# A hybrid decoder layer on one core: the gates of a block regrouped, small PE work queued behind the products before it

## The chip, the cores and the metric

One core of a Trainium2 chip runs the whole program. The metric is the device time of one execution in microseconds (us). Engines are named as in the profile: PE is TensorE (matrix products), DVE is VectorE, ACT is ScalarE, POOL is GpSimd, SP is SyncE, which only issues DMAs here.

## The reference

One layer of a decoder trunk on 1024 prompt tokens and 32 sample tokens, 1056 columns T in all. Two token mixers (latent attention and a state-space layer) run first; then comes the part in question, a gated FFN with a width-3 convolution and a per-layer embedding:

```python
x = x + mixed @ w_out
up = rmsnorm(x, g_ffn) @ w_up                     # 1024 -> 2 x 2816, then a causal conv of width 3
a, v = split(conv(up), 2)
x = x + (gelu(a) * v) @ w_down                    # 2816 -> 1024
x = x + sigmoid(rmsnorm(x, g_ple) @ w_ple_gate) * (p @ w_ple_proj)
```

The last two rows of `up` per sequence are an output of their own (`conv_prompt`, `conv_sample`).

## The kernel before, in words

Everything is kept transposed: 128 channels on the partitions, tokens along the free dimension. Products are made in fp32r, with each operand split into a high and a low part; `mm3` (lines 85 to 88) does three matmuls for one product (high x high, high x low, low x high).

The up projection runs over 22 pairs of row blocks in `up_pair`. Each pair's gelu(a) * v is written to memory (`dhid`, line 2069) and read back later. The last stage is `block(b)` for three blocks of 352 tokens. Each block has a down stage and a gate stage:

- down: 8 outputs `o`, each the sum over 22 hidden row blocks, into a PSUM tile `pd`; `down_out` (lines 2156 to 2167) adds it to the residual `xb`, makes the scaled high and low parts `gg` for the gates, and adds the squares into `sqb`;
- gate: 8 outputs, each 8 row blocks of `gg` times w_ple_gate, 24 matmuls into a PSUM tile `pu`. After gate 0, `sums` (line 2196) adds `sqb` over the partitions with six small matmuls and takes a reciprocal square root; after gate 1, `rows` (line 2208) spreads it along the partitions with three transposes, into `rb`. `rest(o)` (lines 2222 to 2225) multiplies the gate by `rb`, applies the sigmoid, multiplies by `pe` and adds `xb`. `out_turn(o)` (lines 2232 to 2240) transposes the result y with three PE transposes, copies it on ACT and writes it with DMAs from ACT's queue.

The hidden rows of a block arrive as eight pieces h0 to h7 of three row blocks each (h7 has one), loaded from `dhid` and split into `M` tiles by `hid_split` (ACT casts the high part at line 82, DVE or POOL subtracts at line 83). The pieces of block b+1 are split during the gates of block b, piece `o` after gate `o`. The weights come in `raw` tiles of 512 KB (three for a down output, one for a gate output) and are cut into units `wx` of four row blocks, again by ACT and then POOL or DVE by turns. Units are prepared three ahead of the one in use (`ahead`), out of four buffers. Raws of weights and hidden pieces share five buffers: their loads stand in one list (`raw_load`), and each time a raw has been cut, `pull` issues the next load in the list:

```python
        def dn_unit(x):
            kind, o, kg = units[x]
            key = ("d", o, kg // 2) if kind == "d" else ("g", o)
            n = 2 if kind == "d" and kg == 5 else 4
            s = k8()(raws[key])[:, 4 * (kg % 2):4 * (kg % 2) + n]
```

In block 0 the first two down outputs are interleaved: row blocks 0 to 15 of outputs 0 and 1, then the rest of both. `last_rows` (lines 2124 to 2131) makes the conv outputs: four transposes of `LU`, a copy on ACT, two DMAs from ACT's queue; it is called 11 times between down outputs of block 0.

The order on each engine is not the order of the program text: a scheduler puts each instruction on its engine's queue when it counts it as ready, in the order of the text among those that are. `tc.issue_after(ins)` makes what is written in its block stand behind `ins` on that engine's queue. Once queued, instructions of an engine run in their order.

Of the kernel before, what the change touches and what calls it, by code (L numbers as in the profile page):

```python
# [9 lines left out]
F32 = mybir.dt.float32  # L10
# [11 lines left out]
BLK = T // 3  # L22
# [33 lines left out]
def body(tc, I, O):  # L56
# [4 lines left out]
    V, A, G, PE, SP = nc.vector, nc.scalar, nc.gpsimd, nc.tensor, nc.sync  # L61
# [3 lines left out]
    with ctx:  # L65
# [19 lines left out]
        def mm3(out, lh, ll, rh, rl, start, stop_):  # L85
            PE.matmul(out, lh, rh, start=start, stop=False)  # L86
            PE.matmul(out, lh, rl, start=False, stop=False)  # L87
            PE.matmul(out, ll, rh, start=False, stop=stop_)  # L88

        def mm2(out, l2, rh, rl, start, stop_):  # L90

# [769 lines left out]
        for k in range(5):  # L861
            g = gcol["g_cq"][:, k:k + 1] if k < 3 else 1.0
# [247 lines left out]
        for b in range(NB):  # L1110
            o = pt[:HT, b * NT:(b + 1) * NT]
# [569 lines left out]
        def hid_raw(b, g):  # L1681
            n = min(3, NH - 3 * g)
            raw_load(("h", b, g), lambda t: t[:, :n * BLK].rearrange("p (k c) -> p k c", k=n),
                     dhv[:, 3 * g:3 * g + n, b * BLK:(b + 1) * BLK])

        units = []
        for b in range(3):
            kgs = [(o, kg) for o in range(8) for kg in range(6)]
            if b == 0:
                kgs = [(o, kg) for q in (range(4), (4, 5)) for o in range(2) for kg in q] + kgs[12:]  # L1690
            units += [("d", o, kg) for o, kg in kgs] + [("g", o, kg) for o in range(8) for kg in range(2)]

        for b in range(3):
            if b == 0:
                for x in ("h0", (0, 0), "h1", "h2", (0, 1), "h3", "h4", "h5", "h6", (1, 0), (1, 1), (0, 2), "h7", (1, 2)):
                    if x[0] == "h":
                        hid_raw(0, int(x[1]))
                    else:
                        dn_load(*x)
            for o in range(2 if b == 0 else 0, 8):  # L1700
                for i in range(3):
                    dn_load(o, i)
            for o in range(8):
                raw_load(("g", o), k8(), w_pg[:, :, cols_(o)])
                if b < 2:
                    hid_raw(b + 1, o)

        wsum = {}

# [60 lines left out]
        def ahead(n=3):  # L1770
            while wseq and len(wq) < n:
                wq.append(wseq.pop(0)())
# [307 lines left out]
        def hid_split(b, g, eng):  # L2080
            n = min(3, NH - 3 * g)
            hi, lo = (flat(mtile(HB[g] + x))[:, :n * BLK].rearrange("p (k c) -> p k c", k=n) for x in range(2))
            split(raws["h", b, g][:, :n * BLK].rearrange("p (k c) -> p k c", k=n), hi, lo, eng)
            for i in range(n):
                hp_[3 * g + i] = hi[:, i], lo[:, i]
            pull()
# [8 lines left out]
        def last_pair(m):  # L2095
            if m in ORDER[:6]:
                g = ORDER.index(m)
                hid_split(0, g, V if g % 2 else G)
            if m == 4:
                hid_split(0, 6, V)  # L2100

        for j in range(NH):
            up_pair(j, first_pair if j == 0 else last_pair if j == NH - 1 else lambda m: None)
        while post:
            step()
        hid_split(0, 7, V)
        pX.close()
        f1.close()

# [11 lines left out]
        def btile(name, bufs=1, dt=F32):  # L2121
            return p2.tile([128, BLK], dt, name=name, bufs=bufs)

        def last_rows(q):
            pt = ps.tile([128, 512], F32, name="pt")
            for j in range(4):
                PE.transpose(pt[:18, j * 128:(j + 1) * 128], LU[:, q + j], ident)
            lo_ = p2.tile([18, 512], F32, name="lo_", bufs=1)
            A.copy(lo_, pt[:18])
            A.dma_start(cvp[:, q * 128:(q + 4) * 128], lo_[0:2])  # L2130
            A.dma_start(cvs[:, q * 128:(q + 4) * 128], lo_[2:18])

        side = [lambda q=q: last_rows(q) for q in range(0, NH2, 4)]

        def block(b):
            c0 = b * BLK
# [7 lines left out]
                SP.dma_start(xb[o], dx2[cols_(o), c])  # L2144

            def p_in(o):
                pe[o] = btile("pe", 3)
                SP.dma_start(pe[o], dpp[cols_(o), c])

            def down_group(pd, kg):  # L2150
                wt = wq.pop(0)
                ahead()
                for k in range(4 * kg, min(4 * kg + 4, NH)):
                    mm3(pd, wt[:, 0, k % 4], wt[:, 1, k % 4], hp_[k][0], hp_[k][1], k == 0, k == NH - 1)

            def down_out(o, pd):
                V.tensor_tensor(xb[o], pd, xb[o], OP.add)
# [13 lines left out]
            def down(o, kgs):  # L2171
                if 0 in kgs:
                    pds[o] = psd.tile([128, BLK], F32, name="pd")
                for kg in kgs:
                    down_group(pds[o], kg)
                if 5 in kgs:
                    down_out(o, pds.pop(o))
                    if o < 6:
                        x_in(o + 2)
# [3 lines left out]
            if b == 0:  # L2183
                for kgs in (range(4), (4, 5)):
                    for o in range(2):
                        down(o, kgs)
            for o in range(2 if b == 0 else 0, 8):
                down(o, range(6))
                for _ in range(3):
                    if side:  # L2190
                        side.pop(0)()

            def sums():
                pss = ps.tile([128, 512], F32, name="pt")
# [10 lines left out]
            def rows(rst):  # L2205
                pt = ps.tile([128, 512], F32, name="pt")
                for i, (t0, n) in enumerate(TL):
                    PE.transpose(pt[:, t0:t0 + n], rst[:n, i:i + 1].to_broadcast([n, 128]), ident[:n, :n])
                V.tensor_copy(rb, pt[:, :BLK])

            def gate(o):
                pg_ = psu.tile([128, BLK], F32, name="pu")
                for kg in range(2):
                    wt = wq.pop(0)
                    ahead()
                    for k in range(4 * kg, 4 * kg + 4):
                        mm3(pg_, wt[:, 0, k % 4], wt[:, 1, k % 4], GG[k][:, 0], GG[k][:, 1], k == 0, k == 7)
                return pg_

            def rest(o, pg_):  # L2220
                y = Y[o] = btile("y", 3)
                V.tensor_tensor(y, pg_, rb, OP.mult)
                A.activation(y, y, AF.Sigmoid)
                V.tensor_tensor(y, pe[o], y, OP.mult)
                V.tensor_tensor(y, y, xb[o], OP.add)
# [13 lines left out]
                if m < 96:  # L2239
                    A.dma_start(ysv[:, oc], yo[m:96, 2])  # L2240

            pgs = {}
            p_in(0)
            p_in(1)
            for o in range(8):
                pgs[o] = gate(o)
                if b < 2:
                    hid_split(b + 1, o, V)
                if o == 0:
                    rst = sums()  # L2250
                    continue
                if o == 1:
                    rows(rst)
                    rest(0, pgs.pop(0))
                rest(o, pgs.pop(o))
                if o < 7:
                    p_in(o + 1)
                out_turn(o - 1)
            out_turn(7)

        for b in range(3):
# [42 lines left out]
```

## Time and profile before

| | us |
|---|---|
| median of 3 runs | 2055.95 (2052.57 to 2058.73) |
| the profiled execution | 2064.64 |
| its span, first to last instruction | 2062.8 |
| PE busy in the span | 1958.3 (95%) |
| DVE / ACT / POOL busy | 1255.5 / 920.8 / 870.2 |
| mean granted PE clock | 0.968 of full |

Busy times are from one profiled execution. Matmuls overlap each other in the pipeline, so a row of one product shows some 320 ns while the next starts 160 ns later; for the pace of products the starts are compared. The first down product of block 0 starts at 1678.93 us, the gate stages at 1769.15, 1895.83 and 2020.58.

### The profile page before, as it was taken

The numbers are of one execution on the slowest core, as the hardware profiler recorded it, in microseconds if no ns is written. First come the engines' busy times: TensorE is split into PE (matmuls) and PEld (weight loads), VectorE is DVE, ScalarE is ACT, GpSimd is POOL, SyncE is SP. The second block draws the span as 40 slices with busy tenths as digits, with TensorE's granted clock in tenths as the row PEclk, the third lists the DMA queues.
The fourth block names the chain that finished last, engine by engine and source line by source line (L and its number), as shares of the span: only waits on it lengthen the run. The fifth ranks groups of instructions, "written<-read, shape, count | busy, mean of one in ns | idle before, by whom it ended". The sixth has DMA issues, their size and how long they took to land.

```text
span 2062.8 us, 35870 instructions
## 1 busy us (share of the span) xinstructions
PE 1958.3 (95%) x13329; PEld 1839.7 (89%) x13329; DVE 1255.5 (61%) x2467; ACT 920.8 (45%) x1910; POOL 870.2 (42%) x926
## 2 busy tenths in 40 slices
PE   7998999999998989999999899999999989999998
PEld 6897888888777768888999899999999989999998
DVE  6517542335787856565553878787878773734524
ACT  5412332243665544455333454444444454544543
POOL 1106341101323222212442668787878754344342
PEclk9999999998999979999999999999999999999999
DMA  7402221243321100003356432322232274766743
GB/s 250 127 15 59 66 70 55 72 115 110 104 58 45 45 1 12 2 1 139 109 148 214 124 131 63 94 63 94 63 94 63 94 212 139 219 188 180 225 138 102
DMA packets 291927, 211.53 MB, mean 103 GB/s; under 512 B 38417, under 2 KB 273092, under 8 KB 291754
## 3 DMA queue, kind: packets, MB, share of 16 engines
q1 hardware_dynamic: 275102, 195.86, 32.0%
q10 hardware_dynamic: 16652, 13.39, 2.0%
q8 instruction: 105, 1.72, 0.3%
q14 instruction: 68, 0.56, 0.1%
HBM read 161.07 MB, written 46.78 MB: 101 GB/s over the span
## 4 chain that ended last, share of the span: by engine, by line
PE 74%; DVE 10%; ACT 2%; DMA 2%; POOL 2%; issue 2%; SPq 0%; ACTq 0%; DVEq 0%; POOLq 0%
PE q L2014 21%; PE pd L87 4%; PE pd L88 4%; PE pd L86 4%; PE q L1941 3%; PE pm L88 3%; PE pm L87 3%; PE pm L86 3%; PE pt L86 2%; PE pv L1377 2%; PE pt L88 2%; PE pt L87 2%; PE p L86 2%; PE p L88 2%; PE p L87 2%
## 5 line engine op out<-in xcount | busy, mean ns | idle before, releaser
L2014 PE MATMUL q<-M,wx 128*128 128x264 f32 x2112 | 279.2, 285 | 2.0 <-DVE up L2034 2.0
L2014 PEld LDWEIGHTS q<-M,wx 128*128 128x128 f32 x2112 | 266.8, 188 | 2.2 <-issue 2.2
L83 POOL TENSOR_TENSOR wx<-raw,wx 128x512 fp32r<-128x512 f32 x108 | 147.9, 1371 | 226.6 <-ACT wx L82 217.1
L82 ACT CAST wx<-raw 128x512 fp32r<-128x512 f32 x226 | 133.5, 597 | 195.4 <-PE pd L88 117.1
L2014 PE MATMUL q<-P,wx 128*128 128x264 f32 x1584 | 216.0, 285 | 0.1
L2014 PEld LDWEIGHTS q<-P,wx 128*128 128x128 f32 x1584 | 200.3, 188 | 3.8 <-DVE up L2026 3.8
L83 DVE TENSOR_TENSOR wx<-raw,wx 128x512 fp32r<-128x512 f32 (+1 forms) x118 | 92.2, 783 | 141.1 <-ACT wx L82 137.6
L86 PE MATMUL pd<-M,wx 128*128 128x352 f32 x528 | 171.8, 325 | 0.0
L87 PE MATMUL pd<-M,wx 128*128 128x352 f32 x528 | 171.4, 325 | 0.0
L88 PE MATMUL pd<-M,wx 128*128 128x352 f32 x528 | 171.2, 324 | 0.0
L2057 DVE SCALAR_TENSOR_TENSOR cv<-up,cw,cv 128x1024 f32<-128x1024 f32 x88 | 142.1, 1615 | 28.3 <-ACT cv L2049 28.3
L88 PE MATMUL pm<-xh,wl 128*128 128x352 f32 x384 | 126.9, 331 | 0.0
L87 PE MATMUL pm<-xl,wh 128*128 128x352 f32 x384 | 126.5, 329 | 0.0
L86 PE MATMUL pm<-xh,wh 128*128 128x352 f32 x384 | 126.1, 328 | 0.0
L1359 POOL TENSOR_TENSOR Pt<-Pt,mstT 128x128 f32<-128x128 f32 x64 | 30.6, 480 | 176.4 <-ACT Pt L1358 176.4
L86 PEld LDWEIGHTS pd<-M,wx 128*128 128x128 f32 x528 | 100.0, 189 | 0.1
L87 PEld LDWEIGHTS pd<-M,wx 128*128 128x128 f32 x528 | 99.9, 189 | 0.0
L88 PEld LDWEIGHTS pd<-M,wx 128*128 128x128 f32 x528 | 99.9, 189 | 0.0
L1747 ACT CAST wx<-raw 128x512 fp32r<-128x512 f32 x110 | 67.9, 618 | 71.4 <-PE q L2014 46.5
L1941 PE MATMUL q<-M,wx 128*128 128x264 f32 x720 | 90.8, 286 | 5.4 <-POOL wx L83 2.6
L1941 PEld LDWEIGHTS q<-M,wx 128*128 128x128 f32 x720 | 88.3, 188 | 6.8 <-POOL wx L83 3.1
L1748 DVE TENSOR_TENSOR wx<-raw,wx 128x512 fp32r<-128x512 f32 x66 | 76.5, 1159 | 11.8 <-ACT wx L1747 11.8
(705 smaller groups left out, 5473.3 us busy)
## 6 DMA issues: line engine op xcount, KB each, us to landing
raw<-w_down SPq DMA_DIRECT2D x48, 512.0 KB
raw<-w_up SPq DMA_DIRECT2D x44, 512.0 KB
raw<-w_ple_gate SPq DMA_DIRECT2D x24, 512.0 KB
dhid<-cv SPq DMA_DIRECT2D x22, 528.0 KB
raw<-dhid SPq DMA_DIRECT2D x21, 528.0 KB
raw<-w_down SPq DMA_DIRECT2D x24, 384.0 KB
wst<-w_in SPq DMA_DIRECT2D x16, 512.0 KB
cb<-cache_ckv SPq DMA_DIRECT2D x64, 128.0 KB
```

The lines of the kernel that those rows point to most:

```text
L82: A.copy(hi, src)
L83: (eng or G).tensor_tensor(lo, src, hi.bitcast(F32), OP.subtract)
L86: PE.matmul(out, lh, rh, start=start, stop=False)
L87: PE.matmul(out, lh, rl, start=False, stop=False)
L88: PE.matmul(out, ll, rh, start=False, stop=stop_)
L1359: G.tensor_tensor(Pt[:, :128], Pt[:, :128], mstT, OP.add)
L1377: PE.matmul(W["pv"][:, j, :DV + 1], Pts[k][:, q0:q0 + 128], Vb[hp][:, k, e], start=k == 0, stop=k == i)
L1747: A.copy(w[:, 0], s)
L1748: (G if m in (2, 5, 4) else V).tensor_tensor(w[:, 1], s, w[:, 0].bitcast(F32), OP.subtract)
L1941: PE.matmul(p_[:, n, :QW], a_, b_[:, k % 4], start=k + x == 0 and kg == 0, stop=k == 7 and x == 2)
L2014: PE.matmul(o_, l_, r_, start=start and k + x == 0, stop=k + x == 5, skip_group_check=not start)
L2057: V.scalar_tensor_tensor(C[:, :S], U[:, tp:tp + S], w[tp], C[:, :S], op0=OP.mult, op1=OP.add)
```

## The change

The first two gate outputs of a block are made together (first halves of both, then second halves), gate 2 follows, and `sums` and `rows` are queued behind the products of gates 1 and 2. Gates 3 to 5 use the PSUM buffers of the downs. `rest` of the first three outputs follows `rows`; `out_turn` comes two outputs later, behind the products of the gate in front of it. Piece g of the next block is split after gate g + 3, pieces 5 to 7 after the last gate, and the loads are listed in that order. `last_rows` is queued behind the down products in front of it, two calls to an output, with two buffers. In block 0, piece 6 is split one product group later and piece 7 after row blocks 0 to 15 of outputs 0 and 1. `pe` and `y` get four buffers.

```diff
-            units += [("d", o, kg) for o, kg in kgs] + [("g", o, kg) for o in range(8) for kg in range(2)]
+            units += [("d", o, kg) for o, kg in kgs] + [("g", o, kg) for op in ((0, 1), (2,), (3,), (4,), (5,), (6,), (7,)) for kg in range(2) for o in op]
...
                 raw_load(("g", o), k8(), w_pg[:, :, cols_(o)])
-                if b < 2:
-                    hid_raw(b + 1, o)
+                for g in {7: (4, 5, 6, 7)}.get(o, (o - 3,) if o > 2 else ()):
+                    if b < 2:
+                        hid_raw(b + 1, g)
...
-            if m == 4:
+            if m == 3:
                 hid_split(0, 6, V)
...
-        hid_split(0, 7, V)
         pX.close()
...
-            lo_ = p2.tile([18, 512], F32, name="lo_", bufs=1)
+            lo_ = p2.tile([18, 512], F32, name="lo_", bufs=2)
...
-                pe[o] = btile("pe", 3)
+                pe[o] = btile("pe", 4)
...
                     for o in range(2):
                         down(o, kgs)
+                    if 0 in kgs:
+                        hid_split(0, 7, V)
             for o in range(2 if b == 0 else 0, 8):
                 down(o, range(6))
-                for _ in range(3):
+                for _ in range(2):
                     if side:
-                        side.pop(0)()
+                        with tc.issue_after(pe_[0].ins):
+                            side.pop(0)()
...
-            def gate(o):
-                pg_ = psu.tile([128, BLK], F32, name="pu")
+            pgs = {}
+
+            def gate(os_):
+                for o in os_:
+                    pgs[o] = psd.tile([128, BLK], F32, name="pd") if 2 < o < 6 else psu.tile([128, BLK], F32, name="pu")
                 for kg in range(2):
-                    wt = wq.pop(0)
-                    ahead()
-                    for k in range(4 * kg, 4 * kg + 4):
-                        mm3(pg_, wt[:, 0, k % 4], wt[:, 1, k % 4], GG[k][:, 0], GG[k][:, 1], k == 0, k == 7)
-                return pg_
+                    for o in os_:
+                        wt = wq.pop(0)
+                        ahead()
+                        for k in range(4 * kg, 4 * kg + 4):
+                            pe_[0] = mm3(pgs[o], wt[:, 0, k % 4], wt[:, 1, k % 4], GG[k][:, 0], GG[k][:, 1], k == 0, k == 7)
+
+            def held(f, *a):
+
+                with tc.issue_after(pe_[0].ins):
+                    return f(*a)
...
-                y = Y[o] = btile("y", 3)
+                y = Y[o] = btile("y", 4)
...
-            for o in range(8):
-                pgs[o] = gate(o)
-                if b < 2:
-                    hid_split(b + 1, o, V)
-                if o == 0:
-                    rst = sums()
-                    continue
-                if o == 1:
-                    rows(rst)
-                    rest(0, pgs.pop(0))
+            p_in(2)
+            gate((0, 1))
+            rst = held(sums)
+            gate((2,))
+            held(rows, rst)
+            for o in range(3):
                 rest(o, pgs.pop(o))
-                if o < 7:
-                    p_in(o + 1)
-                out_turn(o - 1)
+            for o in range(3, 8):
+                p_in(o)
+                gate((o,))
+                rest(o, pgs.pop(o))
+                rows_in(o - 3)
+                if o == 3:
+                    held(out_turn, 0)
+                held(out_turn, o - 2)
+            rows_in(5)
+            out_turn(6)
+            rows_in(6)
+            rows_in(7)
             out_turn(7)
```

`pe_[0]` is the last product's last matmul, which `mm3` now returns; `rows_in(g)` is `hid_split(b + 1, g, V)` in blocks 0 and 1.

## Rows read from the trace of the kernel before

**Rows 1.** Windows of the last stage: stretch, its length, each engine's busy time, clock, DMA share, GB/s.

```profile
1769.15:1810.72 41.57, 38.00 (x224) 36.56 (x223) 30.66 (x54) 23.61 (x46) 12.58 (x9) 0.92 0.84 241
1810.72:1895.83 85.11, 85.09 (x534) 84.83 (x532) 30.09 (x43) 37.06 (x68) 38.85 (x30) 1.00 0.56 167
1895.83:1934.84 39.01, 35.34 (x225) 33.66 (x223) 30.73 (x53) 22.22 (x45) 11.76 (x8) 1.00 0.90 265
...
2020.58:2055.67 35.09, 34.18 (x221) 33.53 (x220) 21.36 (x45) 14.85 (x34) 9.36 (x7) 1.00 0.36 101
```

**Rows 2.** Waits of PE from 1655 us: us in total, times, longest.

```profile
PE pt L2232 <- DVE y L2225: 5.6, 6, 2.1
PE pt L2127 <- ACT lo__19576 L2129: 4.3, 1, 4.3
PE pt L2196 <- DVE sqb L2167: 2.0, 2, 1.0
...
PE pt L2208 <- DVE rst L113: 0.9, 1, 0.9
```

**Rows 3.** Timeline of PE around the first down product: start, us, instruction, idle before.

```profile
1672.90 1.03 PE L2127 MATMUL pt<-ident,LU 128*18 128x128 f32 x8
1678.26 1.02 PE L2127 MATMUL pt<-ident,LU 128*18 128x128 f32 x4 [4.32 <-ACT lo__19576 L2129]
...
1679.67 0.49 PE L88 MATMUL pd<-M,wx 128*128 128x352 f32 x1
...
1682.89 0.47 PE L87 MATMUL pd<-M,wx 128*128 128x352 f32 x1
```

**Rows 4.** Timeline of DVE in the same stretch.

```profile
1674.28 0.69 DVE L2041 TENSOR_TENSOR up<-q,up 128x528 f32<-128x528 f32 x1
...
1677.77 1.25 DVE L83 TENSOR_TENSOR M<-raw,M 128x1056 fp32r<-128x1056 f32 x1
```

**Rows 5.** Timeline of SP's queue, 1686 to 1698 us.

```profile
1691.72 5.47 SPq L1655 DMA_DIRECT2D raw<-w_down  x5
```

**Rows 6.** Timeline of ACT, 1690 to 1697 us.

```profile
1695.78 1.17 ACT L82 CAST wx<-raw 128x512 fp32r<-128x512 f32 x2 [1.66 <-DMA raw<-w_down]
```

**Rows 7.** Groups by line from 1400 us: count, busy us, mean ns, idle before.

```profile
L83 POOL TENSOR_TENSOR wx<-raw,wx 128x512 fp32r<-128x512 f32 x96 | 131.0, 1365 | 206.4 <-ACT wx L82 197.0 <-DMA xb<-dx 6.0 <-DMA pe<-dpp 3.5
...
L2224 DVE TENSOR_TENSOR y<-pe,y 128x352 f32<-128x352 f32 x24 | 17.3, 726 | 4.7 <-ACT y L2223 4.6
...
L2222 DVE TENSOR_TENSOR y<-pu,rb 128x352 f32<-128x352 f32 x24 | 12.2, 520 | 15.7 <-PE pu L88 15.5
```

**Rows 8.** Timeline of DVE at the first gate products of block 0.

```profile
1770.96 1.26 DVE L83 TENSOR_TENSOR M<-raw,M 128x1056 fp32r<-128x1056 f32 x1 [2.59 <-ACT M L82]
1772.14 0.51 DVE L2157 TENSOR_TENSOR xb<-pd,xb 128x352 f32<-128x352 f32 x1
```

**Rows 9.** Timeline of ACT in the tail, 2051 to 2063 us.

```profile
2056.20 0.37 ACT L2234 COPY yo<-pt 128x256 f32<-128x256 f32 x1 [3.08 <-PE pt L2232]
2056.47 0.50 ACT L2223 ACTIVATE y<-y 128x352 f32<-128x352 f32 x1
...
2057.84 0.59 ACTq L2240 DMA_DIRECT2D y_sample<-yo  x1
2058.78 0.37 ACT L2234 COPY yo<-pt 128x256 f32<-128x256 f32 x1 [1.49 <-PE pt L2232]
```

**Rows 10.** Timeline of SP's queue over block 1's gate stage, 1876 to 1936 us.

```profile
1879.73 0.37 SPq L1655 DMA_DIRECT2D raw<-dhid  x1
...
1900.37 0.37 SPq L1655 DMA_DIRECT2D raw<-dhid  x1
...
1918.02 0.38 SPq L1655 DMA_DIRECT2D raw<-w_down  x1
```

**Rows 11.** Timeline of ACT over the same stretch.

```profile
1904.73 1.07 ACT L82 CAST M<-raw 128x1056 fp32r<-128x1056 f32 x1 [2.59 <-DMA raw<-dhid]
...
1929.30 0.62 ACT L82 CAST wx<-raw 128x512 fp32r<-128x512 f32 x1 [1.25 <-DMA raw<-w_down]
```

**Rows 12.** Windows of five us over the same stage, the busiest of eight.

```profile
1930.00:1935.00 5.00, 5.00 (x35) 4.96 (x34) 2.45 (x5) 2.26 (x6) 1.29 (x2) 1.00 1.14 334
```

More of the change, by code (lines that the diff above doesn't have):

```diff
@@ L87, in mm3 @@
             PE.matmul(out, lh, rl, start=False, stop=False)
-            PE.matmul(out, ll, rh, start=False, stop=stop_)
+            return PE.matmul(out, ll, rh, start=False, stop=stop_)
         def mm2(out, l2, rh, rl, start, stop_):
@@ L2133, in body @@
         side = [lambda q=q: last_rows(q) for q in range(0, NH2, 4)]
+        pe_ = [None]
         def block(b):
@@ L2153, in down_group @@
                 for k in range(4 * kg, min(4 * kg + 4, NH)):
-                    mm3(pd, wt[:, 0, k % 4], wt[:, 1, k % 4], hp_[k][0], hp_[k][1], k == 0, k == NH - 1)
+                    pe_[0] = mm3(pd, wt[:, 0, k % 4], wt[:, 1, k % 4], hp_[k][0], hp_[k][1], k == 0, k == NH - 1)
             def down_out(o, pd):
@@ L2240, in out_turn, with rows_in @@
                     A.dma_start(ysv[:, oc], yo[m:96, 2])
-            pgs = {}
+            def rows_in(g):
+                if b < 2:
+                    hid_split(b + 1, g, V)
             p_in(0)
             p_in(1)
-            for o in range(8):
-                pgs[o] = gate(o)
-                if b < 2:
-                    hid_split(b + 1, o, V)
-                if o == 0:
-                    rst = sums()
-                    continue
-                if o == 1:
-                    rows(rst)
-                    rest(0, pgs.pop(0))
-                rest(o, pgs.pop(o))
-                if o < 7:
-                    p_in(o + 1)
-                out_turn(o - 1)
+            p_in(2)
[4 more added lines that the diff above has]
+            for o in range(3):
+                rest(o, pgs.pop(o))
+            for o in range(3, 8):
[10 more added lines that the diff above has]
+            rows_in(7)
             out_turn(7)
```

## The prediction

> **What bounds the kernel now.** I read the table of the whole execution first: TensorE is busy 95% of the span, so time can only come out of the stretches in which it waits or runs at the half clock, and out of the tail. Second, the windows of the last stage [rows 1]. A gate stage is the same 192 products in every block. It takes 35.1 us in block 2, where nothing is loaded for a later block, but 41.6 us in block 0 and 39.0 us in block 1. Third, TensorE's waits from 1655 us on [rows 2]: four of its rows make 12.8 us: transposes waiting for y, the first rows of LU, the sums of squares, the row factors. Last, the queues around them.
>
> The pace of a product comes from block 1's downs: 85.11 us for 528 products and a few transposes, 0.161 us each [rows 1]. At the half clock eleven starts span 3.22 us, 0.293 us each [rows 3].
>
> **Part 1, the start of the downs (LU rows queued behind products, pieces 6 and 7 later).** Eight LU transposes run at 1672.90, then TensorE idles 4.32 us until ScalarE has copied their result, four more follow, and the first down product starts at 1678.93 [rows 3]. Behind the products they can't do that. What the first product then waits for is the old PSUM bank, which VectorE empties at 1674.28 + 0.69 = 1674.97 [rows 4]: 3.96 us earlier. The 12 transposes now cost their 0.13 us each among products (eight took 1.03 us): +1.5, so -2.5. The half clock that follows the idle time (15 products, 15 x 0.132 = 2.0 us) may stay, since 2.0 us of idleness remain.
>
> What is late next is a weight: the third raw of output 1 is queued on SP behind piece 7, which waits for the last hidden rows. It goes out at 1691.72 [rows 5] and is cast at 1695.78 [rows 6]; with the cast's 0.62 and GpSimd's 1.37 us for the low half [rows 7] it is ready near 1697.8. Its products now come 114 products after 1678.93, 15 cold and 99 warm, at 1699.3: 1.5 us of slack. Piece 6's split (1.25 us on VectorE at 1677.77 [rows 4]) moves behind the last eviction of the up stage, so that chain comes 1.25 us earlier. The gain is thus 0 to 3 us, at most 4.7 if the loads change order; I take -2.4. LU's two side calls for three, and the second `lo_`, cost nothing: ScalarE has room there, and the transposes are the same 44.
>
> **Part 2, gates 0 and 1 together, then 2, then sums and rows.** Now the last output's eviction sits behind a hidden split on VectorE that waited 2.59 us for ScalarE's cast (1770.96), and begins only at 1772.14, after that split's 1.26 us, while the gate products run [rows 8]. TensorE waits for its gg parts, then for the sum of squares (twice 1.0 us), then for the row factors (0.9 us) [rows 2]. With 24 more products before the last slice is due (12 x 0.161 = 1.9 us) and before the sums (3.9 us), these waits are covered, and with them the half clock that follows them in block 0 (mean clock 0.92 against 1.00 [rows 1]). The hidden pieces no longer sit there, since the first now follows gate 3. Evictions of three outputs wait together for the rows; six PSUM banks by turns hold them, so the products don't wait.
>
> Block 2's stage shows the floor: 35.1 us, with one output's three transposes fewer inside (0.4 us by the same row). So block 0 can give 41.57 - 35.09 - 0.4 = 6.1 us and block 1 3.5 us. Two more waits of transposes lie outside these differences, one inside the floor and one past block 1's stage; I put them at 0.7 us each, the mean of the five that are not the tail's, (5.6 - 2.1) / 5 [rows 2]. With y two outputs old they go. Sum -11.0 us.
>
> **Part 3, what these moves add.** After the rows three evictions come at once: per output 0.52 + 0.73 us [rows 7] and an add like the first, 5.3 us for three on VectorE, against gate 3's 3.9 us. Transposes 0 and 1 stand behind gate 3, and output 1 may be late by 0 to 1.3 us in each block: +1.5 in all (0 to 4).
>
> The tail gets one output more on ScalarE. From 2056.20 to 2057.84 + 0.59 = 2058.43 it holds one output's copies and three issues, 1.83 us without the sigmoid, and starts the last one at 2058.78 [rows 9]. Its slack of 0.35 us can't hold another 1.83: +1.5, less 0.4 of transposes that leave the products: +1.1 (0 to 1.4).
>
> **Part 4, the loads at the end of a gate stage.** This is the disputed cost. Five `raw` buffers serve weights and hidden pieces in one order. Now four loads of the next block's pieces go out before the first gate product, the first at 1879.73 against 1895.83, three of them early enough to have all but landed by then, and the next block's first weight goes out at 1918.02, 16.8 us before its stage [rows 1, 10]. After the change all eight pieces follow gate 3's weight, so that weight comes after h0 to h7 and g4 to g7. There is also one buffer fewer. When gate 6's second unit prepares down unit (0,0), pieces 3 to 7 hold all five buffers; the dictionary's key ("d", 0, 0) has no block in it, so the unit is cut from the old block's raw (the same weights), which must be kept since that block's first down. The new raw is then kept likewise.
>
> The pace of loads in the gates: from h4 at 1900.37 to that weight at 1918.02 seven further loads, 2.5 us each [rows 10]. With the first one going out some 1 us after the first gate product (gate 0's buffer, freed one unit later), the thirteenth, the new weight, goes out at 1 + 12 x 2.5 = 31 us. A load lands 4.4 us after its issue (h4, cast at 1904.73), or 11.3 us (that weight, cast at 1929.30) [rows 10, 11]. Cut in 2.0 us, it is ready 37 to 44 us after the first gate product. The undisturbed stage lasts some 34 us (block 2's 35.09 less a wait of its own) and the unit cut from the kept raw covers 1.9 us more: TensorE waits 1 to 8 us at the start of blocks 1 and 2, with clock loss behind it if it idles as long as at 1678. I take 4 + 2.0 = 6 us, nearer to the h rows, of which there are more: +12 in all (2 to 20).
>
> The bytes say the same. 39.01 us at 265 GB/s are 10.3 MB [rows 1]; three pieces of 0.53 MB more make 11.9 MB, in 34 us 350 GB/s, above the busiest five us (334 GB/s, share 1.14) [rows 12]; at that rate they take 35.6 us, at block 1's mean 45.
>
> The Trainium skill, "DMA: Bandwidth & Descriptors", section "Specifications", gives about 358 GB/s as a core's limit at the memory, with which 11.9 MB would need 33 us and there would be no wait. No row here sustains that; it is the rival "loads in time" below.
>
> **Sum.** -11.0 - 2.4 + 1.5 + 1.1 + 12 = +1.2 us. The profiled execution took 2064.64 us (span 2062.8 and 1.8 around it), so 2065.8; the median of the runs shown is 8.7 us lower, 2055.95, and I put the same change on it: 2057.
>
> **Rivals.** *Given back at the next block* (the sum; 0.38): -11 to -14 us in the gates and the start, returned as a wait on a raw at the first downs of blocks 1 and 2. For it: the saturated DMA share at 1930; against it: some transfers (outputs, xb, pe) also move later and need not be in time. *Loads in time* (0.35): hidden pieces are split as soon as they land, so buffers cycle faster and the weight lands before 34 us; boundary cost 2 us in all, -8.8 us, 2047. For it: ScalarE is busy only 57% of block 1's gate stage, so a split can follow its landing [rows 1]. *Late raws, slower* (0.27): landing takes 11 us as that one weight did, each boundary costs 8 + 2 us, +9.2 us, 2065; it decides from a wait of 6.5 us per boundary on, where with the clock's 2.0 the two make 17 us and the sum passes +6.2. Cast waits that block ScalarE's queue in front of weight casts would push the same way. *The queueing does nothing*, because transposes wait as before: then only the start's -2.4 and the tail's +1.1 us remain, -1.3, inside the first case's chance.
>
> **Numbers.** 0.3% is 6.2 us, about what a measurement of this kernel can tell from no change. Faster holds the second case, 0.35; same 0.38; slower 0.27. The likeliest is 2057; its own range is 2050 to 2062. For 8 in 10 I reach from 2043 (start and gates in full, little returned) to 2068 (20 us at the boundaries).
>
> **What would show it.** Right: no LU transpose before the first down product, and that one near 1675; no TensorE wait at sums and rows; gate stages of 34 to 36 us; then a wait at the second unit of blocks 1 and 2 that ends with a cast after a raw of w_down; a down unit 0 cast long before its block's other weights' landing. Wrong: gate stages of 34 us and no wait behind them (then 2043 to 2047), or waits inside the gates on casts (then above 2062).

## The result: 0.5% slower, and the profile after

The changed kernel takes 2067.01 us (median of 6 runs, 2064.83 to 2073.1), the kernel before 2055.8 in the same series: ratio 1.0052, 95% interval 1.0034 to 1.007, some 11 us slower. The forecast was 2057 with a range of 2043 to 2068; the time lies at its upper end, near the 2065 of the rival "late raws, slower" (chance 0.27), but, as the rows show, only in part for that rival's reason.

I compare the two profiled executions from one point on, the start of the last 48 matmuls of the up stage (1666.99 us before, 1660.84 after), since the earlier stages have nothing to do with the change. A product is here one matmul of 352 columns; the half clock is a granted clock of 0.5, at which a product takes 0.29 us and not 0.16. Each column is the difference of two starts of stages in the trace: start to the first gate product of block 0; gates of block 0 with the downs of block 1; gates of block 1 with the downs of block 2; gates of block 2 and the tail.

| us | start + downs 0 | gates 0 + downs 1 | gates 1 + downs 2 | gates 2 + tail | sum |
|---|---|---|---|---|---|
| before | 102.16 | 126.68 | 124.75 | 42.22 | 395.81 |
| after | 103.06 | 129.08 | 129.57 | 43.15 | 404.86 |
| difference | +0.90 | +2.40 | +4.82 | +0.93 | +9.05 |

The windows of the stages of the changed kernel, in the columns of [rows 1] (gates 0, downs 1, gates 1, downs 2, gates 2 with the tail), and the waits of TensorE from 1655 us on, which answer to [rows 2]:

```profile
1763.90:1802.20 38.30, 34.49 (x224) 33.85 (x222) 29.48 (x52) 22.23 (x42) 11.56 (x8) 1.00 0.80 242
1802.20:1893.00 90.80, 87.29 (x535) 86.43 (x534) 29.07 (x44) 38.54 (x73) 38.54 (x31) 0.98 0.56 164
1893.00:1931.50 38.50, 34.60 (x224) 33.75 (x223) 30.62 (x53) 21.69 (x41) 11.84 (x8) 1.00 0.81 242
1931.50:2022.60 91.10, 87.98 (x534) 87.37 (x533) 27.41 (x42) 37.45 (x71) 38.63 (x31) 0.96 0.57 165
2022.60:2065.70 43.10, 34.94 (x226) 34.09 (x224) 22.49 (x48) 16.42 (x39) 9.02 (x7) 0.96 0.32 87
```

```profile
PE pt L2245 <- DVE y L2238: 15.7, 8, 3.0
PE pd L88 <- DVE wx L83: 2.2, 1, 2.2
PE pd L86 <- DVE up L2042: 2.0, 1, 2.0
PE q L2015 <- DVE up L2035: 2.0, 1, 2.0
PE pd L86 <- ACT wx L82: 0.9, 1, 0.9
```

The waits at LU, at the sums and at the row factors are gone, as forecast. In their place the transposes of y (line 2245) wait 15.7 us, against 5.6 before. The gate stages got shorter by 3.2 and 0.5 us, and the downs of blocks 1 and 2 longer by 5.6 and 5.4 us. Three places make this up.

**The start.** Timeline of TensorE:

```profile
1660.84 3.15 PE L2015 MATMUL q<-M,wx 128*128 128x264 f32 x24 [1.96 <-DVE up L2035]
...
1668.93 0.40 PE L86 MATMUL pd<-M,wx 128*128 128x352 f32 x1 [2.01 <-DVE up L2042]
...
1670.18 0.49 PE L87 MATMUL pd<-M,wx 128*128 128x352 f32 x1
...
1673.41 0.36 PE L86 MATMUL pd<-M,wx 128*128 128x352 f32 x1
...
1679.06 0.43 PE L88 MATMUL pd<-M,wx 128*128 128x352 f32 x1 [2.21 <-DVE wx L83]
```

and of VectorE in front of the last of these rows:

```profile
1674.57 1.27 DVE L2058 SCALAR_TENSOR_TENSOR cv<-up,cw,cv 128x1024 f32<-128x1024 f32 x1
1675.77 0.24 DVE L2059 SCALAR_TENSOR_TENSOR cv<-ub,cw,cv 128x32 f32<-128x32 f32 x1
1675.93 2.31 DVE L2058 SCALAR_TENSOR_TENSOR cv<-up,cw,cv 128x1024 f32<-128x1024 f32 x1
1678.16 0.24 DVE L2059 SCALAR_TENSOR_TENSOR cv<-ub,cw,cv 128x32 f32<-128x32 f32 x1
1678.32 1.28 DVE L83 TENSOR_TENSOR wx<-raw,wx 128x512 fp32r<-128x512 f32 x2
```

The first down product starts 8.09 us after the common point, where it took 11.94 before: 3.85 us earlier (3.96 forecast). But the low half of the fourth unit stands on VectorE behind the whole convolution, TensorE waits 2.21 us for it, and a second run of 11 products at the half clock follows (1680.54 to 1683.76). One operation of the convolution takes 2.31 us there, beside a split of GpSimd that runs from 1675.87 to 1677.16, where the same operation takes 1.27 just before: 1.04 us longer, about half of the wait.

**The row factors and the first y.** VectorE in the gates of block 0, from the row factors to the first two y:

```profile
1777.58 0.52 DVE L2214 COPY rb<-pt 128x352 f32<-128x352 f32 x1
1778.02 1.34 DVE L83 TENSOR_TENSOR wx<-raw,wx 128x512 fp32r<-128x512 f32 x1
1779.28 1.37 DVE L2235 TENSOR_TENSOR y<-pu,rb 128x352 f32<-128x352 f32 x3
1780.92 1.26 DVE L83 TENSOR_TENSOR M<-raw,M 128x1056 fp32r<-128x1056 f32 x1 [0.27 <-ACT M L82]
1782.73 0.96 DVE L2237 TENSOR_TENSOR y<-pe,y 128x352 f32<-128x352 f32 x2 [0.55 <-ACT y L2236]
1783.61 0.95 DVE L2238 TENSOR_TENSOR y<-y,xb 128x352 f32<-128x352 f32 x2
```

From the rows' copy to the first y are 6.5 us (1784.13), to the second 7.0; gate 3 lasts 3.9. The transposes behind it wait 2.31 us here, 2.95 in block 1 and 0.82 in block 2. On the way to the first y are a unit of weights (1.34 us, beside a split of GpSimd, where it takes 0.69 alone) and then ScalarE, which casts a late piece and loads a table before the first sigmoid:

```profile
1779.82 1.08 ACT L82 CAST M<-raw 128x1056 fp32r<-128x1056 f32 x1 [2.40 <-DMA raw<-dhid]
1780.91 1.28 ACT L2236 ACT_TABLE_LOAD   x1
1782.20 1.27 ACT L2236 ACTIVATE y<-y 128x352 f32<-128x352 f32 x3
```

VectorE's own split of the piece (1780.92) falls into this time and costs nothing here. In block 1 it stands between the multiplication and the addition of the first y (1910.68), and the addition, beside a split of GpSimd, takes 1.59 us for 0.52. In block 2, which has no pieces and no table load there, the wait of 0.82 us is no longer than what GpSimd adds: a multiplication of 0.52 us takes 1.35 beside its split.

```profile
2037.93 1.32 POOL L83 TENSOR_TENSOR wx<-raw,wx 128x512 fp32r<-128x512 f32 x1 [2.89 <-ACT wx L82]
2038.28 1.35 DVE L2237 TENSOR_TENSOR y<-pe,y 128x352 f32<-128x352 f32 x1 [0.19 <-ACT y L2236]
```

**The block boundary.** Gate 7's last product starts at 1799.80. VectorE behind it, in order, then two rows of TensorE:

```profile
1802.94 1.26 DVE L83 TENSOR_TENSOR M<-raw,M 128x1056 fp32r<-128x1056 f32 x1 [1.14 <-ACT M L82]
1805.33 0.69 DVE L83 TENSOR_TENSOR wx<-raw,wx 128x512 fp32r<-128x512 f32 x1 [1.12 <-ACT wx L82]
1805.93 0.52 DVE L2235 TENSOR_TENSOR y<-pu,rb 128x352 f32<-128x352 f32 x1
1806.37 0.52 DVE L83 TENSOR_TENSOR M<-raw,M 128x352 fp32r<-128x352 f32 x1
1807.89 1.29 DVE L2237 TENSOR_TENSOR y<-pe,y 128x352 f32<-128x352 f32 x1 [1.01 <-ACT y L2236]
1809.22 0.52 DVE L2238 TENSOR_TENSOR y<-y,xb 128x352 f32<-128x352 f32 x1
```

```profile
1805.35 0.43 PE L86 MATMUL pd<-M,wx 128*128 128x352 f32 x1 [0.94 <-ACT wx L82]
...
1809.89 0.76 PE L2245 MATMUL pt<-ident,y 128*128 128x128 f32 x3 [2.43 <-DVE y L2238]
```

The last output could be evicted at 1800.1, but stands on VectorE behind the split of a piece and of a weight that both wait for casts of late raws; it begins at 1805.93. Its transposes, queued among the first down products, then hold TensorE for 2.43 us (2.98 at the next boundary), those of output 6 for 1.50 (0.95), and the half clock follows both times. The first weight of block 1 goes out at 1798.57 and is cast at 1804.68.

### The profile page after: what moved, and what is told of

The parts are those of the page before. It is cut to its first block, busy times and chain, and to the rows that moved or that the text cites. A ratio compares the mean times of both kernels' runs of the same rounds, so it can differ in the third digit from the quotient of the medians.

```text
span 2065.7 us, 35827 instructions
## 1 busy us (share of the span) xinstructions
PE 1953.7 (95%) x13329; PEld 1837.5 (89%) x13329; DVE 1246.6 (60%) x2467; ACT 920.1 (45%) x1910; POOL 868.5 (42%) x926
## 4 chain that ended last, share of the span: by engine, by line
PE 77%; DVE 10%; DMA 4%; ACT 3%; issue 2%; POOL 2%; SPq 1%; ACTq 0%; POOLq 0%; DVEq 0%
PE q L2015 21%; PE pd L88 4%; PE pd L87 4%; PE pd L86 4%; PE pm L87 4%; PE pm L88 4%; PE pm L86 4%; PE q L1942 3%; PE pt L86 3%; PE pt L88 2%; PE pv L1377 2%; PE pt L87 2%; PE p L86 2%; PE p L88 2%; PE p L87 2%
## 5 line engine op out<-in xcount | busy, mean ns | idle before, releaser
L86 PE MATMUL pd<-M,wx 128*128 128x352 f32 x528 | 174.5, 330 | 3.0 <-DVE up L2042 2.0
L88 PE MATMUL pd<-M,wx 128*128 128x352 f32 x528 | 173.3, 328 | 2.5 <-DVE wx L83 2.2
L87 PE MATMUL pd<-M,wx 128*128 128x352 f32 x528 | 173.3, 328 | 0.0
L86 PEld LDWEIGHTS pd<-M,wx 128*128 128x128 f32 x528 | 101.8, 193 | 3.6 <-issue 2.2
L88 PEld LDWEIGHTS pd<-M,wx 128*128 128x128 f32 x528 | 101.6, 192 | 3.4 <-DVE wx L83 3.4
L87 PEld LDWEIGHTS pd<-M,wx 128*128 128x128 f32 x528 | 101.7, 193 | 0.0
```

Of the source, the lines that this page charges most:

```text
L88: return PE.matmul(out, ll, rh, start=False, stop=stop_)
```

## Experiments

All are compared with the kernel before; "of after" means against the changed kernel's 1.0052. The columns are those of the table above, from one profiled execution each. How much one execution says can be seen from run 5, which changes nothing behind the first downs: its two middle columns lie 2.5 and 2.0 us under after's, for the greater part because no product there runs at the half clock (after has 11 and 17 such products, 1.5 and 2.2 us). A difference of about 2 us in one column is not read without its rows.

| run | ratio, 95% interval | start + downs 0 | gates 0 + downs 1 | gates 1 + downs 2 | gates 2 + tail |
|---|---|---|---|---|---|
| 1 turns of 6, 7 later | 1.0021 (1.0008 to 1.0035) | 103.30 | 127.94 | 125.58 | 43.06 |
| 2 pieces as before | 1.0007 (0.9996 to 1.0018) | 103.70 | 121.88 | 130.56 | 43.07 |
| 3 turns of 0, 1 later | 1.0036 (1.0024 to 1.0047) | 103.16 | 128.13 | 128.42 | 42.90 |
| 4 start as before | 1.0032 (1.002 to 1.0044) | 102.12 | 129.64 | 130.96 | 43.07 |
| 5 unit 3 on GpSimd | 1.0029 (1.0013 to 1.0045) | 101.13 | 126.55 | 127.56 | 43.14 |
| 6 = 2, even pieces on GpSimd | 1.0052 (1.0035 to 1.0068) | 102.95 | 126.03 | 134.70 | 43.05 |
| 7 even pieces on GpSimd | 1.0066 (1.0043 to 1.0089) | 102.82 | 135.11 | 133.47 | 43.13 |
| 8 = 1 + 2 + 5 + 7 | 1.0037 (1.0019 to 1.0055) | 100.29 | 125.34 | 134.09 | 43.10 |
| 9 = 2 + 4, gates alone | 1.0024 (1.0015 to 1.0034) | 101.76 | 126.76 | 128.77 | 43.14 |
| 10 = 1 + 2 + 5 | 0.9978 (0.9966 to 0.9991) | 100.95 | 120.90 | 127.33 | 43.15 |
| 11 = 10, rows first | 0.997 (0.9952 to 0.9987) | 100.97 | 122.38 | 122.80 | 43.16 |
| 12 = 11, short tail | 0.9966 (0.9949 to 0.9983) | 101.25 | 122.36 | 123.76 | 42.06 |

**Run 1, the last transposes of a block behind the next downs.**

```diff
-            out_turn(6)
...
-            out_turn(7)
+            for o in (6, 7):
+                if b < 2: late.append(lambda o=o: out_turn(o))
+                else: out_turn(o)
...                                      # in the next block, behind down(0) and down(1)
+                if late:
+                    with tc.issue_after(pe_[0].ins):
+                        late.pop(0)()
```

> The changed kernel, except that in blocks 0 and 1 the transposes of the last two outputs, 6 and 7, are queued behind the first and the second down output of the next block, not in front of its first products. Theory 'queue order': at each block boundary TensorE loses its time at these transposes alone (waits of 1.50 and 2.43 us and about 1.2 us of half clock at the first boundary, 0.95 and 2.98 us and about 2.0 us of half clock at the second, and 0.3 us for each of four groups of transposes that move into the downs without a wait); with them out of the way it gains 11 us or a little more, and the whole change comes out equal to the kernel before. Rival 'late loads': the weight itself is late. The second unit of the first down output could not start before 1805.35 us in the first boundary, so the 1.50 us come back as a longer wait there, and in the second boundary about 1 us likewise; the gain is then 5 to 9 us, and the profile shows a wait of 2.5 to 3.5 us that ends with a cast of wx.

It gained 6.4 us of after (0.0031 x 2056; the two intervals just touch). The two boundaries differ. At the second the full price of the transposes came back (-4.0 us). At the first only 1.1 us did, and TensorE waits for weights instead:

```profile
1800.95 0.43 PE L86 MATMUL pd<-M,wx 128*128 128x352 f32 x1 [2.07 <-ACT wx L82]
...
1804.57 0.43 PE L86 MATMUL pd<-M,wx 128*128 128x352 f32 x1 [1.02 <-ACT wx L82]
...
1805.92 0.43 PE L88 MATMUL pd<-M,wx 128*128 128x352 f32 x1 [0.76 <-POOL wx L83]
```

So at the first boundary the loads are late, as the rival says, and the y waits had hidden it.

**Run 2, pieces loaded and split as before.**

```diff
-                for g in {7: (4, 5, 6, 7)}.get(o, (o - 3,) if o > 2 else ()):
-                    if b < 2: hid_raw(b + 1, g)
+                if b < 2: hid_raw(b + 1, o)
...
-                rows_in(o - 3)
+                rows_in(o)             # 0, 1 after gates 0 and 1, 2 after gate 2
```

> The changed kernel with the hidden pieces loaded and split as in the kernel before, one behind each gate output in the list of loads, and nothing else undone. Theory 'late pieces': the last y of a block is late because VectorE's queue holds it behind splits of pieces and of a weight that land late; with the pieces early, the down stages of blocks 1 and 2 go back from 91 to 85 or 86 us and the kernel gains 9 to 11 us, while the gate stages change by less than 2 us. Rival 'queue order alone': the transposes stand in front of the down products whatever is loaded, y is late by VectorE's three evictions that wait for the rows, and the gain is below 3 us. A third way: the pieces' splits take VectorE's time in front of the rows again, and the gate stages get longer by 3 us or more each.

It gained 9.3 us of after. Block 0 with its boundary falls by 7.2 us, to 121.88, 4.8 under the kernel before: late pieces and late weights were that boundary's cost. Block 1 does not gain (+1.0): the third way happened there. VectorE between the sums and the row factors of block 1, GpSimd beside it, and TensorE's wait for them:

```profile
1898.48 0.17 DVE L99 TENSOR_SCALAR rf_i<-msx 128x3 int32<-128x3 int32 x1
1898.56 1.26 DVE L83 TENSOR_TENSOR M<-raw,M 128x1056 fp32r<-128x1056 f32 x1
1899.74 1.24 DVE L100 TENSOR_SCALAR rf_i<-rf_i 128x3 int32<-128x3 int32 x1
```

```profile
1899.60 1.36 POOL L83 TENSOR_TENSOR wx<-raw,wx 128x512 fp32r<-128x512 f32 x1 [1.83 <-ACT wx L82]
```

```profile
PE pt L2212 <- DVE rst L113: 3.1, 1, 3.1
```

A piece sits inside the chain of small operations that makes the row factors, and holds it for 1.2 us. The next of them, L100, shows 1.24 us, though it is an operation of 0.17: the piece is done at 1899.82, but GpSimd's split runs until 1900.96, and L100 ends at 1900.98. So the chain lost about as much to the work of GpSimd as to the piece.

**Run 3, transposes 0 and 1 behind gate 4.**

```diff
-                if o == 3:
-                    held(out_turn, 0)
-                held(out_turn, o - 2)
+                if o == 4:
+                    held(out_turn, 0)
+                    held(out_turn, 1)
+                if o > 3: held(out_turn, o - 2)
...
-                y = Y[o] = btile("y", 4)
+                y = Y[o] = btile("y", 5)
```

> The changed kernel with the transposes of outputs 0 and 1 queued behind gate 4 and not gate 3, and five buffers of y for four. Theory: the waits of 2.31, 2.95 and 0.82 us in the three gate stages are late rows, and one gate more in front of the transposes covers them: 6 us less, and the half clock is not touched. Rival: VectorE is behind for the whole stage, so the wait only moves to the next transposes; then 2 us or less.

3.3 us of after by the times, 2.3 by the table: between the two. The waits behind gate 3 are gone, but in block 0 the transposes behind gate 4 now wait 3.14 us for an instruction of VectorE (by the profile a weight's split), in block 1 1.68 us for ScalarE's copy.

**Run 4, the old start.** LU not held, three calls to an output, pieces 6 and 7 where they were.

> The changed kernel with the start of the downs as in the kernel before: the LU rows not queued behind products, three to an output, one buffer, pieces 6 and 7 split where they were. By the forecast the new start gains 2.4 us, so this kernel would be 2.4 us slower than the changed one. By the trace of the changed kernel the 3.9 us by which the first product comes earlier are lost again at the fourth unit, whose low half stands on VectorE behind the convolution (a wait of 2.21 us and the half clock behind it, and twelve more transposes among the products), so this kernel would be equal or up to 1.5 us faster.

Its first column is 0.9 us lower than after's, so no gain of the new start shows; the times say 4 us, with intervals that overlap after's. The middle columns of its profile are 0.6 and 1.4 us higher, which was not followed up. Times and first column point against the forecast's -2.4.

**Run 5, one instruction of the start on another engine.**

```diff
-            split(s, w[:, 0, :n], w[:, 1, :n], V if x % 2 else G)
+            split(s, w[:, 0, :n], w[:, 1, :n], V if x % 2 and x != 3 else G)
```

> The changed kernel with one instruction moved: the low half of the fourth unit of the first down stage is cut on GpSimd, which idles there for 3.0 us, and not on VectorE, where it stands behind the convolution. Theory: this one instruction gives back the gain of the new start; the wait of 2.21 us and the half clock behind it (11 products, 11 x 0.13 = 1.4 us) go, 3.6 us less. Rival: the sixth unit, also on VectorE behind the convolution, takes its place, or piece 7 does, and the gain is 0 to 1.5 us.

The wait of 2.21 us is gone; four waits of 0.56 to 0.76 us at later units take a part of its place. First column 101.13, 1.9 us under after's, between the theory's 3.6 and the rival; by the times the gain is 4.7 us of after, with overlapping intervals. Runs 10 to 12, which contain this edit, show 100.95 to 101.25 too, some 1 us under before's 102.16. But their first downs have no product at the half clock, and before's have 15 (2.0 us): that the new start gives anything beyond a better draw of the clock is not shown.

**Runs 6 and 7, the even pieces on GpSimd.** Run 6 on top of run 2, run 7 on the changed kernel.

```diff
-                    hid_split(b + 1, g, V)
+                    hid_split(b + 1, g, V if g % 2 else G)
```

> The second experiment's kernel (pieces loaded and split as before the change), and the even pieces are split on GpSimd, 2.48 us each and not 1.26 us on VectorE. In the second experiment block 1 lost 3.10 us at the row factors and 1.45 us at a unit of weights, with the half clock behind it, where block 0 lost only 0.29 us. Theory: there VectorE was behind because four pieces were split in front of the rows; with half of them on GpSimd, which is busy for 12 of 38 us, these waits go and block 1 gains 5 to 6.5 us over the second experiment: about 6 us faster than the kernel before. Rival: GpSimd's longer splits hold the buffers, and its own units of weights come late; then no gain, or a few us slower.

> The changed kernel with the even pieces split on GpSimd. Theory 'VectorE is behind': the waits behind gate 3 (2.31 and 2.95 us) have one split of 1.26 us in front of y, and the last y of a block has two; 4 to 8 us less. Rival 'late loads': at the block boundaries the splits wait for landings and so does the first weight; only the waits behind gate 3 shrink, 1.3 us each, 2.5 us less in all, and the second unit of block 1 still waits for its cast.

No gain: run 6 is 9.3 us slower than run 2, and run 7 no faster than after (its interval overlaps after's; by the table it is 9.7 us slower). Run 6 loses at the row factors of both blocks, 3.28 and 5.04 us. A row of GpSimd and one of VectorE in its block 1 show what happens:

```profile
1903.76 2.43 POOL L83 TENSOR_TENSOR M<-raw,M 128x1056 fp32r<-128x1056 f32 x1 [1.93 <-ACT M L82]
```

```profile
1904.23 2.51 DVE L83 TENSOR_TENSOR wx<-raw,wx 128x512 fp32r<-128x512 f32 x1 [1.31 <-ACT wx L82]
```

VectorE's subtraction of 0.69 us took 2.51 and ended 0.55 us after GpSimd's: moving a split of 1.26 us to GpSimd cost VectorE more than doing it. What these splits cost in all is seen from runs 8 and 10 below, which differ in nothing else.

**Run 8, four edits together.**

> The grouped and held gates kept, and four edits together: the pieces loaded and split as before the change, the even ones on GpSimd, the transposes of outputs 6 and 7 behind the first two down outputs of the next block, and the fourth unit of the first down stage cut on GpSimd. If the four causes are separate, the stages from the last up product on are 95.0 (start and first downs), 122 and 122 (gates and downs) and 43 us, 382 us against 391.4 us in the profile of the kernel before: 9 us faster, near 2047. If they share one cause, the best single experiment is the bound: equal to the kernel before.

It missed by 17 us (7.6 slower than before, where 9 faster was expected): it contains the splits on GpSimd, and loses 3.32 and 4.99 us at the row factors. The late transposes work: its downs of blocks 1 and 2 take 85.2 and 85.3 us.

**Run 9, the gates alone.** Runs 2 and 4 together, so only the regrouped, held gates remain.

> The kernel before with the regrouped and held gates alone: pieces loaded and split as before, the start of the downs as before. It shows what part 2 and part 3 of the forecast are worth without part 1 and part 4; by the forecast -11.0 + 1.5 + 1.1 = -8.4 us. By the second experiment's profile (gates and next downs 121.9 and 130.6 us, where the kernel before had 126.7 and 124.8) it is worth nothing, -1 to +3 us: what block 0 gains, block 1 loses at the row factors.

4.9 us slower than before. With the old start VectorE's order in block 0 changed too, and now both blocks wait for the row factors (3.09 and 3.13 us) and for a weight in the gates (1.38 and 1.61 us). The regrouping by itself moves the waits; it does not remove them.

**Run 10, runs 1, 2 and 5 together, all splits on VectorE.**

> The second experiment's kernel (pieces as before the change) with the transposes of outputs 6 and 7 behind the next block's first downs and the fourth unit of the first down stage on GpSimd; all pieces' splits stay on VectorE. If the two edits keep the prices that they had alone (3.6 us at the start; 1.9 us and 1.4 us of half clock at block 1's boundary), 6 to 7 us under the second experiment: 4 to 6 us faster than the kernel before. Rival: the splits on GpSimd were not what cost time in the eighth run, and this kernel is as slow as that one, 1.003 to 1.005 of the kernel before.

4.5 us faster than before, as expected, and 12 us faster than run 8, whose only difference is the even pieces on GpSimd. The largest wait left is that for block 1's row factors (3.14 us, with 16 products at the half clock); a unit of weights in front of it (1.63) and one y of block 0 (1.65) are left too.

**Run 11, no piece in front of the row factors.**

```diff
             gate((2,))
-            rows_in(2)
-            held(rows, rst)
+            rb_ = held(rows, rst)
+            rows_in(2)
...                                      # in rows_in, pieces 2 to 7
+                    with tc.issue_after(rb_.ins):
+                        hid_split(b + 1, g, V)
```

> The same kernel, and the VectorE splits of pieces 2 to 7 queued behind the copy of the row factors, so that no split stands in front of them. Theory: block 1's wait of 3.10 us at the row factors and its half clock (16 products, 2.1 us) were VectorE's order alone and go: 4 to 6 us under the kernel without this edit, 8 to 11 us faster than the kernel before. Rival: pieces held back keep their raw buffers, so the loads behind them and the first weight of the next block come later, and the wait shows up again at a unit of weights in the gates or at the second unit of the next downs: no gain, or slower.

6.2 us faster than before; by the table 3.0 under run 10, less than the expected 4 to 6, and by the times 1.6, which is not told from no change. What the trace shows is the wait: TensorE now stands 0.88 us at block 1's row factors, without the half clock behind it, and block 1 with its boundary falls by 4.5, from 127.33 to 122.80; block 0 rises by 1.5. Windows of gates 0, downs 1, gates 1 and downs 2:

```profile
1756.40:1793.30 36.90, 34.97 (x222) 33.48 (x220) 26.70 (x49) 21.06 (x40) 10.90 (x8) 1.00 0.76 226
1793.30:1878.70 85.40, 85.40 (x536) 85.14 (x535) 33.34 (x48) 38.81 (x73) 39.89 (x30) 1.00 0.65 187
1878.70:1916.30 37.60, 34.88 (x221) 33.49 (x220) 29.68 (x51) 21.02 (x42) 11.07 (x8) 1.00 0.78 223
1916.30:2001.50 85.20, 85.20 (x537) 85.17 (x536) 27.80 (x44) 36.37 (x70) 38.40 (x30) 1.00 0.58 171
```

The downs are back at the pace of [rows 1], and the clock is full in all four.

**Run 12, the tail.** In the last block the transposes of outputs 5 and 6 come one gate earlier.

> The kernel of the eleventh run, and in the last block the transposes of outputs 5 and 6 one gate earlier, so that only output 7 is left behind the last product, as before the change. Theory (part 3 of the forecast): the tail is one or two outputs' copies and DMA issues on ScalarE, about 1.9 us for one (its last output is copied at 2039.45 us in the eleventh run, and one output's copies and issues in front of it begin at 2037.54); the last stage of the profile is 1.0 to 1.9 us shorter than its 43.2 us. Rival: the end is set by the last y, for which TensorE waits 1.74 us in every run, and by the last DMA, and the stage stays within 0.3 us. In the whole time it is below what can be told.

The last stage is 1.1 us shorter, 42.06 (1.0 by the last instructions' ends, since a span is printed to 0.1 us). This version has the lowest ratio of the study, 0.9966 of the kernel before, 7 us, and some 18 us under the changed one; from run 11 it is not told apart.

## Why the forecast was too low, step by step

| term | forecast | measured |
|---|---|---|
| part 1, start | -2.4 | +0.9 |
| parts 2, 3 (without the tail) and 4: gates and boundaries | -11.0 + 1.5 + 12 = +2.5 | +7.2 |
| tail | +1.1 | +0.9 |
| sum | +1.2 | +9.05 |

The time came near the third rival's 2065 partly by luck: that rival puts 20 us at the two boundaries, where some 12.5 were, and the rest came from the start and from y, for which the forecast had a gain and a small price.

**Part 1 failed at "what is late next".** The gain of 3.96 us at the first product was right to 0.1 us. The next late thing I looked for was a raw behind SP's queue, at 1697.8, 30.8 us behind the common point; it was a unit whose raw had long landed, behind the convolution on VectorE, 17.5 us behind the common point (1678.32 less 1660.84). Run 5 shows that it was this instruction. [Rows 4] show VectorE up to 1677.77 with the products starting at 1678.93; with them 4 us earlier, VectorE's list should have been read unit by unit against their new starts. The +0.9 adds up to within 0.2 us: 3.85 us earlier, 2.21 of a new wait, 1.5 (the forecast's price) for twelve transposes among the products, and 22 products at the half clock where 15 were (0.9).

**Part 2 was right on what vanishes, too high on what is left.** All the named waits went. But the changed kernel has no gate stage of 34 to 36 us: 38.3 and 38.5. Block 0 came near it in runs 1, 2 and 10 (36.1, 36.1 and 35.6), block 1 in none; run 11 has 36.9 and 37.6, with waits of 0.5 to 1.0 us left in them. Run 11's two columns are together 6.3 us under the kernel before, where -11.0 + 1.5 = -9.5 was forecast.

**Part 3's y was mis-sized.** I counted three evictions, 5.3 us, against gate 3's 3.9, and took 0 to 1.3 us a block, 1.5 in all. The three waits are 2.31 + 2.95 + 0.82 = 6.1 us. Left out were what stands between the rows' copy and the first y besides the evictions: a weight's split, ScalarE's cast of a late piece (1.08 us in blocks 0 and 1), its table load in block 0 (1.28), a piece's split on VectorE in block 1 (1.25), and that VectorE's operations take longer beside GpSimd's splits (0.65 us for the weight in blocks 0 and 1, 1.07 for the addition in block 1, 0.83 for the multiplication in block 2). Block 2, without pieces, shows the 0.82 that was in my range. The size of the tail was right, and run 12 gives it back.

**Part 4 was right in size and half right in mechanism.** The forecast put the new weight's issue 31 us after the first gate product and its use at 37 to 44 us; measured are 34.7 (1798.57) and 41.5 (1805.35), and the second unit of block 1 waits on a cast, as named. But the wait there is only 0.94 us, because TensorE was held up by y already. What I left out is who else stands behind a late raw: the last y on VectorE, and behind it transposes queued in front of down products. The waits at the two boundaries (1.50 + 0.94 + 2.43 and 0.95 + 2.98) and the half clock behind them (11 and 17 products, 1.5 and 2.2) make some 12.5 us, against 12 forecast. Run 2 shows late pieces as the cause at the first boundary, run 1 the transposes' place at the second.

The Trainium skill's limit of about 358 GB/s ("DMA: Bandwidth & Descriptors", section "Specifications") stood for "loads in time". No run here shows that rate in a gate stage: 242 GB/s after, and 223 to 226 in run 11, where no unit of the next downs waits. The order of the loads decided, not the rate.

Left open: whether the raw buffer that is kept for the old block's first weight matters by itself was not tried, and the price of part 1 by time alone (run 4) is known only to some 3 us.

## What to carry to other kernels

A small piece of work that is queued in front of the next stage's products puts its whole producer chain on TensorE's path: read the producer's queue up to that instruction, and see which entry there waits for a transfer. Bringing a start forward is worth as much as the instructions that feed the following units, on every engine, come forward with it. A short serial chain, such as the row factors, wants nothing in front of it that can wait for a load; held free of that, with the last transposes of a block behind the next block's products and one unit of the start on GpSimd, the same regrouping was 0.3% faster and not 0.5% slower. And a free GpSimd is no free place for such a split while VectorE has work: the trace shows VectorE's rows grow beside it.

## What was not expected of the hardware

VectorE's subtraction of two operands in SBUF does not run beside GpSimd's: 0.69 us alone, 2.51 us when GpSimd's split of 2.43 us had begun 0.47 us before it. In the changed kernel, from 1650 us on, each of the 30 weight splits of VectorE that begin while a split of GpSimd runs ends 0.55 us behind it, however long it has stood; the other 42 take 0.68 to 0.70 us. The Trainium skill, "SBUF: two separate sides" in "SBUF — State Buffer", describes this as an exclusive lock of a shared pair of ports, held for the whole instruction by whichever starts first; the rows agree.

A wait of one length is followed by the half clock in one execution and not in another. In the changed kernel 2.01 us of idleness at 1668.93 are followed by 11 products at 0.29 us each (1670.18 to 1673.41). In run 10 a wait of 2.02 us at the same product is not: the products behind it start 0.16 us apart.

```profile
1673.07 0.40 PE L86 MATMUL pd<-M,wx 128*128 128x352 f32 x1 [2.02 <-DVE up L2041]
```

In run 5 waits of 1.55 and 3.14 us at the second boundary (1922.28 and 1928.34) are not either, and no product of its downs and of its gates in blocks 0 and 1 runs at the half clock. So the 1 to 2 us of half clock behind a wait of this length came in some executions and not in others, and one profile shows only one draw of it.
